# A decoder step on one Trainium2 core: the layer norm's offset added where Z is read, a pair's finish in two steps, four output jobs together

## The chip, the core and the metric

The kernel runs on one core of one Trainium2 chip. Its time is device microseconds of one execution; the profile is of one execution more. TensorE multiplies, VectorE and ScalarE read its results out of PSUM (eight banks of 128 x 512 fp32) and prepare the operands, GpSimd and SyncE issue transfers.

## The reference, cut to what matters

A trunk of two layers over 544 tokens: 512 of a prompt and 32 of eight samples. Each layer is an FFN, a mixer (retention in layer 0, an RG-LRU in layer 1) and a second FFN, and after each of the three stands a layer norm with scale and offset.

```python
def swiglu(x, w_in, w_out):
    g, u = jnp.split(x @ w_in, 2, axis=-1)
    return (jax.nn.silu(g) * u) @ w_out
...
    for layer in range(DEPTH):
        x = layer_norm(ALPHA * x + 0.5 * swiglu(x, ffn1_w_in[layer], ffn1_w_out[layer]),
                       ln_g[layer, 0], ln_b[layer, 0])
        ...  # m = retention (layer 0) or RG-LRU (layer 1)
        x = layer_norm(ALPHA * x + m, ln_g[layer, 1], ln_b[layer, 1])
        x = layer_norm(ALPHA * x + 0.5 * swiglu(x, ffn2_w_in[layer], ffn2_w_out[layer]),
                       ln_g[layer, 2], ln_b[layer, 2])
```

D_MODEL is 1024, D_FF 2816, ALPHA the fourth root of 4; everything is fp32.

## The kernel before

**Layout.** Everything lies transposed: features on the partitions, tokens along the free axis, in two halves of 272 tokens. x has 8 chunks of 128 features. `Z` holds x in fp32; `X`, in the large tile BIG, holds it as a high and a low f32r part (`X[:, 0]`, `X[:, 1]`). A product is three matmuls (`mm3`, line 359): high by high, weight's low by high, high by x's low. Weights come in blocks of 128 x 1024 fp32 (eight tiles) by DMA into one of six `raw` buffers; ScalarE copies the high part into an `hl` buffer and VectorE writes the low part (a split, `split`). There are six `hl` buffers; two more places (`ext`) serve only the plain jobs named below.

**Order of work.** The Python program keeps a clock of its own for TensorE, ScalarE and VectorE (`Flow`, `fl`). Work for the last two is written as generators that yield an event or a time; the next of them to be due is issued when TensorE's planned time passes it. `pace()` is such a time: TensorE's now, or 0.8 us before the later of the other two is through with what it has. So the order of the instructions on each engine is fixed when the program is built, and every engine then runs its own list in that order. `pump` puts in weight splits as buffers come free and blocks have landed.

**An FFN** (`ffn`, called with g = 0, 2, 3 and 5; the two mixers are g = 1 and 4) cuts the 22 chunks of its hidden size into three parts of 8, 8 and 6. The first four chunks of part 0 are plain jobs: gate and up products of each half of the tokens, `ev_g` and `ev_u` read them out of PSUM. All further chunks go in pairs of two chunks by two halves with seven products where eight would be plain (`pair`): the forms s1, a11, s2, a12, s3, s4, a22, in this order, each for gate (i = 0) and up (i = 1), 12 matmuls for each i. The forms s1, s2, s3 and a22 multiply sums and differences of the blocks of x; `sums()` makes them from `Z`, in 1088-wide steps (4 chunks of 272). The generator `ev` combines the products as they end, in the tiles GT and UT (four stretches of 272: chunk j half 0, chunk j half 1, chunk j+1 half 0, chunk j+1 half 1) and RT. `finish` then takes SiLU of the last three stretches of GT in one instruction (816 wide), multiplies with UT in another, and writes the high and low part of both chunks of the hidden state H, 1088 wide each. `hf` says that this is done; the next pair waits for it before it writes GT and UT again.

**Output jobs.** After the pairs of a part come its 16 output jobs, one for each chunk m of x and each half: 8 (in part 2: 6) products over the part's chunks of H. `gangs(jobs, 2)` runs the first two of them interleaved, a product of one, then of the other; all others run alone. `zev` reads a job's bank and adds it to `Z`: in part 0 as ALPHA * Z + bank. In part 2 the job of m = 0 also gives a shift, the sum over chunk 0 of Z (two fp32 matmuls at line 363 for each half), and `prep` subtracts it from the other seven chunks; sums for mean and variance then follow job by job, and `ln` normalises a half after its last job. In part 2 the last four chunks of half 0 come before those of half 1 (in the last FFN, seven), so that half 1's jobs run beside half 0's norm.

**The norm's end.** `ln` writes Z * scale * rstd to `Z`, then with the offset added the two parts of `X`, chunk by chunk. Behind that, for g = 1, 2, 3 and 5, a loop adds the offset to `Z` itself, with a ScalarE instruction for each chunk and half (lines 685 to 691, the event `xf`) and a `pace()` before each. `sums()` of an FFN waits for all 16 of these, and part 0's `zev` for that of its chunk.

`lru_rates` makes the RG-LRU's rates out of `lam`: a few operations of 10 columns on ScalarE, one of them an Exp, and some 30 on VectorE. It stands ahead of FFN 3 and comes due 60 us after that.

Of the kernel before, what the change touches and what calls it, by code (L numbers as in the profile page):

```python
# [27 lines left out]
KC = DM // P  # L28
T = 512
# [174 lines left out]
def build(tc, D, O):  # L204
# [42 lines left out]
    def ccol(name, i=0, w=1, rows=P):  # L247
        return CT[0:rows, CC[name] + i:CC[name] + i + w]

    ident = ccol("ident", 0, P)  # L250
# [139 lines left out]
    def pace():  # L390
        return max(fl.pe, max(fl.dve, fl.act) - 0.8)
# [216 lines left out]
    def ln(li, half, g, final, dep, flush):  # L608
# [75 lines left out]
        fl.set(("lnd", g, half), fl.pe)  # L684
        if not final and g != 4:

            for c in range(KC):
                yield pace()
                z = Z[:, c, sl]
                t = act(z, z, dep=fl.ev["x", g, c, half], func=AF.Identity, bias=pcol("ln_b", 8 * li + c))  # L690
                fl.set(("xf", g, c, half), t)

    def zev(m, half, first, last, lnargs, count, guard=()):
# [4 lines left out]
        def prep(first):  # L698

            for c in range(1, KC):  # L700
                z = Z[:, c, sl]
                if first:
                    t = act(z, f(X[:, 0, c, sl]), scale=ALPHA)
                    stt(z, f(X[:, 1, c, sl]), ALPHA, z, ALU.mult, ALU.add, dep=t)
                else:
                    yield ("zp", g, c, half)
                tt(z, z, L.SH[:, sl], ALU.subtract)
                fl.set(("zd", g, c, half), fl.dve)
                yield pace()
# [26 lines left out]
        def ev(b, t):  # L736
# [10 lines left out]
            if first and not last:  # L747
                yield ("xf", g - 1, m, half)
                t = stt(z, z, ALPHA, b[:, :HF], ALU.mult, ALU.add, dep=t)
                release(b, t)  # L750
            elif first and not m:
                t = stt(z, f(X[:, 0, m, sl]), ALPHA, b[:, :HF], ALU.mult, ALU.add, dep=t)
                release(b, t)
                t = stt(z, f(X[:, 1, m, sl]), ALPHA, z, ALU.mult, ALU.add)
            else:
                t = tt(z, z, b[:, :HF], ALU.add, dep=t)
                release(b, t)
# [85 lines left out]
    def ffn(l, w, g, final=False, extra=None):  # L843
# [47 lines left out]
        def sums():  # L891

            yield ("lnd", g, 1) if g else 0.0
            for c in range(KC):
                for half in range(2):
                    yield ("xf", g, c, half)
            o = LNB[g].o
            T = ar(o, 3, HK * HF).rearrange("p i (c n) -> p i c n", c=HK)
            b11, b12, b21, b22 = (Z[:, k:k + HK, h * HF:h * HF + HF] for k in (0, HK) for h in (0, 1))

            def parts(name, src, hi, lo, t):
# [4 lines left out]
            t = tt(T[:, 0], b11, b12, ALU.subtract)  # L906
            t1 = tt(T[:, 1], b12, b22, ALU.subtract)
            parts("s1", T[:, 0], TF[:, 0, 0], TF[:, 0, 1], t)
            yield pace()
            t = tt(T[:, 2], b11, T[:, 1], ALU.subtract)  # L910
            parts("s2", T[:, 2], TF[:, 1, 0], TF[:, 1, 1], t)
            yield pace()
            parts("s3", T[:, 1], TF[:, 2, 0], TF[:, 2, 1], t1)
            yield pace()
            t = tt(T[:, 0], b21, T[:, 2], ALU.subtract)
            yield ("plain", nin)
# [10 lines left out]
        def pair(j, units_of, p):  # L927
# [6 lines left out]
            def ev(form, i, b, t):  # L934
# [17 lines left out]
                elif form == "s3":  # L952
                    yield ("rd", nin, j, "s4", i)
                    t = tt(B1[i], b, B1[i], ALU.subtract, dep=t)
                    fl.set(("rd", nin, j, "a22", i), t)
                elif form == "a22":
                    t = tt(A1[i], b, R[i], ALU.subtract, dep=t)
# [22 lines left out]
            def finish():  # L980
                for i in range(2):
                    for k in ("c12", "c21"):
                        yield (k, nin, j, i)
                    yield ("rd", nin, j, "a22", i)
                    if i == 0:
                        ts = act(GT[:, HF:], GT[:, HF:], dep=fl.ev["c21", nin, j, 0], func=AF.Silu)
                yield ("h11", nin, j)
                t = stt(UT[:, HF:], UT[:, HF:], 0.5, GT[:, HF:], ALU.mult, ALU.mult, dep=ts)
                hh, hl = H[:, 0, c:c + 2], H[:, 1, c:c + 2]
                u2 = UT.rearrange("p (c n) -> p c n", c=2)  # L990
                t = act(hh, u2, dep=t)
                t = tt(hl, u2, f(hh), ALU.subtract, dep=t)
                for m in (j, j + 1):
                    for half in range(2):
                        fl.set(("h", nin, m, half), t)
                fl.set(("hf", nin, j), t)
# [48 lines left out]

        if extra:
            do(extra)
        do(lambda: st.update(ext=(2, 3)))
        do(lambda: fl.spawn(sums()))
        for hf, (j0, j1) in enumerate(PARTS):  # L1050
# [14 lines left out]
            for m, half in ab(list(range(KC)), (7 if final else 4) if hf == 2 else 0):  # L1065
                def rhs(k, half, j0=j0):
# [3 lines left out]
                                zev(m, half, hf == 0, hf == 2, (li, g + 1, final), count, guard)))  # L1070
            gangs(jobs, 2)

# [525 lines left out]
    def lru_rates():  # L1598
# [5 lines left out]
        def gen():  # L1604
            yield fl.pe + 60
            act(e, lam, func=AF.Abs)
# [208 lines left out]
    with tc.manual_schedule():  # L1815
        def load():
# [22 lines left out]
            def xsplit(c, half, dep):  # L1839
# [3 lines left out]
                fl.set(("x", 0, c, half), t)  # L1843
                fl.set(("xf", 0, c, half), t)
            for c in range(KC):
# [8 lines left out]
            def rest():  # L1854
# [8 lines left out]
                for c in range(KC):  # L1863
                    xsplit(c, 1, 0.0)
                    yield pace()
            fl.spawn(rest())
        load()
# [110 lines left out]
```

## Time and profile before

| | |
|---|---|
| median of 3 runs | 2351.94 us (2349.43 to 2356.76) |
| profiled execution, its own time | 2353.06 us |
| its span, first to last instruction | 2351.3 us |
| TensorE busy | 2289.0 us, 97% |
| VectorE busy | 1532.3 us, 65% |
| ScalarE busy | 1021.0 us, 43% |
| mean granted TensorE clock | 0.991 |

The span is what the trace shows; the profiled execution's own time has 1.8 us more around it. Times in the rows below are microseconds from the span's start. A bracket behind a row of a timeline holds the idle time ahead of it on that engine, and what ended it. The half and the full clock are 0.5 and 1 in the column of the granted clock.

### The profile page before, as it was taken

What the parts mean: (1) busy time and instruction counts of PE and PEld (TensorE: products, weight loads), DVE (VectorE), ACT (ScalarE), POOL (GpSimd) and SP (SyncE); (2) the same over time, 40 slices, a digit from 0 to 9 for tenths busy, and PEclk for the clock granted to TensorE, in tenths of its full rate; (3) what the DMA queues carried; (4) which work ended last, traced back from release to release, by engine and by line L of the source; (5) the groups of instructions that cost most, each with busy time, mean ns of one, the idle gap of its engine ahead of it and who ended that gap; (6) DMA issues with size and microseconds to landing.
All of it is one profiled execution on the core that took longest, in us unless ns stands there. A gap on an engine that the chain in (4) does not pass through costs nothing.

```text
span 2351.3 us, 41831 instructions
## 1 busy us (share of the span) xinstructions
PE 2289.0 (97%) x17530; PEld 2238.5 (95%) x17530; DVE 1532.3 (65%) x2630; ACT 1021.0 (43%) x1557; POOL 143.5 (6%) x195
## 2 busy tenths in 40 slices
PE   9999999999999999999999989999999999999997
PEld 9999999989899998999999989999999999999996
DVE  6647368776766677764636865564787678646367
ACT  5424244442434335533424453333458846424243
POOL 0011000000000000001110000101011000011000
PEclk9999999999999999999999989999999999999998
DMA  7667562153342544466756336665412233657551
GB/s 218 180 140 178 118 178 73 57 174 120 134 159 99 167 144 135 107 162 140 193 113 165 91 84 159 160 172 126 135 59 90 90 108 97 179 117 186 126 139 39
DMA packets 89485, 312.29 MB, mean 133 GB/s; under 512 B 9760, under 2 KB 13856, under 8 KB 89296
## 3 DMA queue, kind: packets, MB, share of 16 engines
q1 hardware_dynamic: 68016, 232.06, 30.0%
q0 software_dynamic: 21280, 77.56, 19.4%
q8 instruction: 137, 2.24, 0.4%
q14 instruction: 52, 0.43, 0.1%
HBM read 288.29 MB, written 21.29 MB: 132 GB/s over the span
## 4 chain that ended last, share of the span: by engine, by line
PE 89%; DVE 7%; ACT 3%; issue 1%; DMA 0%; SPq 0%; ACTq 0%; DVEq 0%
PE bank L359 87%; DVE hl L320 1%; PE bank L363 1%; ACT hl L301 1%; ACT BIG L301 1%; DVE ARF L320 1%; DVE BIG L320 1%; DVE ARF L324 1%; DVE Z L324 1%; DVE Z L320 1%; ACT ARF L301 0%; DVE ARF L329 0%; DVE BIG L324 0%; DVE SM L338 0%; PE bank L367 0%
## 5 line engine op out<-in xcount | busy, mean ns | idle before, releaser
L359 PE MATMUL bank<-BIG,hl 128*128 128x272 f32 x15096 | 1949.7, 290 | 44.0 <-ACT BIG L301 18.9
L359 PEld LDWEIGHTS bank<-BIG,hl 128*128 128x128 f32 x15096 | 1920.5, 189 | 63.9 <-ACT BIG L301 22.7
L320 DVE TENSOR_TENSOR hl<-raw,hl 128x1024 fp32r<-128x1024 f32 (+1 forms) x490 | 596.1, 1221 | 493.6 <-ACT hl L301 491.0
L301 ACT ACTIVATE hl<-raw 128x1024 fp32r<-128x1024 f32 (+1 forms) x490 | 514.1, 1055 | 751.3 <-PE bank L359 572.1
L301 ACT ACTIVATE BIG<-ARF 128x272 fp32r<-128x272 f32 (+11 forms) x198 | 124.0, 638 | 231.9 <-DVE ARF L324 136.5
L464 POOL DMA_DIRECT2D raw<-in_win x144 | 125.5, 899 | 1425.5 <-DVE hl L320 756.5
L320 DVE TENSOR_TENSOR BIG<-ARF,BIG 128x272 fp32r<-128x272 f32 (+11 forms) x198 | 136.6, 702 | 103.2 <-ACT BIG L301 102.6
L320 DVE TENSOR_TENSOR ARF<-bank,ARF 128x272 f32<-128x272 f32 (+3 forms) x460 | 186.0, 436 | 14.6 <-PE bank L363 7.9
L359 PE MATMUL bank<-BIG 128*128 128x272 f32 (+5 forms) x1172 | 194.1, 316 | 0.2 <-DVE ARF L329 0.2
L359 PEld LDWEIGHTS bank<-BIG 128*128 128x128 f32 (+3 forms) x1172 | 167.9, 188 | 13.8 <-DVE ARF L329 0.7
L320 DVE TENSOR_TENSOR Z<-Z,bank 128x272 f32<-128x272 f32 (+1 forms) x238 | 115.0, 491 | 63.4 <-PE bank L359 55.1
L359 PE MATMUL bank<-hl,BIG 128*128 128x256 f32 (+2 forms) x1024 | 146.6, 300 | 2.7 <-ACT BIG L301 1.9
L301 ACT ACTIVATE ARF<-bank 128x272 f32<-128x272 f32 (+5 forms) x278 | 108.9, 400 | 82.6 <-PE bank L359 42.1
L359 PEld LDWEIGHTS bank<-hl,BIG 128*128 128x128 f32 (+1 forms) x1024 | 127.3, 179 | 13.9 <-ACT BIG L301 2.1
L301 ACT ACTIVATE ARF<-Z 128x272 f32<-128x272 f32 (+1 forms) x86 | 39.4, 458 | 103.8 <-DVE Z L320 101.1
L320 DVE TENSOR_TENSOR ARF<-ARF 128x272 f32<-128x272 f32 (+1 forms) x146 | 61.4, 445 | 3.4 <-ACT ARF L301 1.4
L301 ACT ACTIVATE BIG<-Z,PR 128x272 fp32r<-128x272 f32 x80 | 40.8, 521 | 40.6 <-DVE Z L324 40.6
L320 DVE TENSOR_TENSOR Z<-Z,ARF 128x272 f32<-128x272 f32 (+1 forms) x116 | 50.4, 473 | 9.5 <-ACT ARF L301 9.0
L301 ACT ACTIVATE ARF<-ARF 128x272 f32<-128x272 f32 (+1 forms) x79 | 48.3, 631 | 0.4
L324 DVE SCALAR_TENSOR_TENSOR Z<-Z,bank 128x272 f32<-128x272 f32 x80 | 34.3, 434 | 20.4 <-PE bank L359 20.2
L324 DVE SCALAR_TENSOR_TENSOR raw<-raw,bank 128x512 f32<-128x512 f32 x64 | 41.0, 682 | 9.0 <-PE bank L359 9.0
L324 DVE SCALAR_TENSOR_TENSOR ARF<-ARF,PR 128x512 f32<-128x512 f32 (+1 forms) x92 | 40.6, 497 | 9.2 <-ACT ARF L301 9.0
(79 smaller groups left out, 665.0 us busy)
## 6 DMA issues: line engine op xcount, KB each, us to landing
raw<-in_win SPq DMA_DIRECT2D x173, 512.0 KB, 4.3
raw<-in_win POOLq DMA_DIRECT2D x144, 512.0 KB, 5.7
raw<-in_wout SPq DMA_DIRECT2D x88, 512.0 KB, 4.4
raw<-in_sret SPq DMA_DIRECT2D x32, 512.0 KB, 3.6
out_rets<-raw SPq DMA_DIRECT2D x32, 512.0 KB, 5.1
raw<-in_rwin_v SPq DMA_DIRECT2D x16, 512.0 KB, 3.6
raw<-in_rwin_kq SPq DMA_DIRECT2D x16, 512.0 KB, 4.0
raw<-in_rwin_g SPq DMA_DIRECT2D x16, 512.0 KB, 4.7
```

The source lines that it names most:

```text
L301: nc.scalar.activation(out=out, in_=in_, func=func, scale=scale, **kw)
L320: nc.vector.tensor_tensor(out=out, in0=a, in1=b, op=op)
L324: nc.vector.scalar_tensor_tensor(out=out, in0=a, scalar=s, in1=b, op0=op0, op1=op1)
L359: nc.tensor.matmul(out, lhsT=a, rhs=b, start=start, stop=stop, skip_group_check=cont)
L363: nc.tensor.matmul(out, lhsT=a, rhs=b, start=start, stop=stop)
L464: nc.gpsimd.dma_start(out=u["raw"], in_=ap, accum_op=ALU.add)
```

## The change

`Z` now stays without the offset. `offsets()` fills a new tile LB at the start with ALPHA times each norm's offset, and with the offset's chunks 0 to 3 minus its chunks 4 to 7. Whoever reads `Z` adds what is missing: `prep` and the m = 0 job of part 2 ALPHA times the offset (`alb`), `sums()` the offset or the difference, chunk by chunk in instructions of 272 columns (`minus`). The 16 instructions at the end of `ln` and the event `xf` are gone; `sums()` waits for the end of the norm.

`finish` has two steps. The first, when c12 is there (after s4), makes half 1 of chunk j, and with half 0 its two parts of H, 544 columns wide. The second, when c21 and c22 are there (after a22), does the same for chunk j+1. `gangs` interleaves four output jobs in place of two. `lru_rates` is put between the pairs and the output jobs of part 0, and comes due 12 us after that.

```diff
         return CT[0:rows, CC[name] + i:CC[name] + i + w]
+    LB = sbt("LB", 72)
+    def offsets():
+        lb = PR[:, PC["ln_b"]:PC["ln_b"] + 48]
+        tsc(LB[:, 0:48], lb, ALPHA, ALU.mult)
+        l3 = lb.rearrange("p (l a c) -> p l a c", l=6, a=2)
+        tt(LB[:, 48:72].rearrange("p (l c) -> p l c", l=6), l3[:, :, 0], l3[:, :, 1], ALU.subtract)
+    def alb(g, c):
+        return LB[:, 8 * (g - 1) + c:8 * (g - 1) + c + 1]
...
         fl.set(("lnd", g, half), fl.pe)
-        if not final and g != 4:
-            for c in range(KC):
-                yield pace()
-                z = Z[:, c, sl]
-                t = act(z, z, dep=fl.ev["x", g, c, half], func=AF.Identity, bias=pcol("ln_b", 8 * li + c))
-                fl.set(("xf", g, c, half), t)
...
                     yield ("zp", g, c, half)
-                tt(z, z, L.SH[:, sl], ALU.subtract)
+                if first or g == 1:
+                    tt(z, z, L.SH[:, sl], ALU.subtract)
+                else:
+                    stt(z, z, alb(g - 1, c), L.SH[:, sl], ALU.add, ALU.subtract)
                 fl.set(("zd", g, c, half), fl.dve)
...
             if first and not last:
-                yield ("xf", g - 1, m, half)
                 t = stt(z, z, ALPHA, b[:, :HF], ALU.mult, ALU.add, dep=t)
...
                 t = stt(z, f(X[:, 1, m, sl]), ALPHA, z, ALU.mult, ALU.add)
+            elif last and not m and g > 1:
+                t = stt(z, z, alb(g - 1, 0), b[:, :HF], ALU.add, ALU.add, dep=t)
+                release(b, t)
             else:
...
-            yield ("lnd", g, 1) if g else 0.0
-            for c in range(KC):
-                for half in range(2):
-                    yield ("xf", g, c, half)
+            yield ("lnd", g, 1) if g else ("x", 0, KC - 1, 1)
             o = LNB[g].o
...
             b11, b12, b21, b22 = (Z[:, k:k + HK, h * HF:h * HF + HF] for k in (0, HK) for h in (0, 1))
+            c0 = 8 * (g - 1)
+            def minus(out, x, bias, y):
+                if not g:
+                    return tt(out, x, y, ALU.subtract)
+                for c in range(HK):
+                    i = 48 + HK * (g - 1) + c
+                    s = LB[:, i:i + 1] if bias < 0 else pcol("ln_b", c0 + bias + c)
+                    t = stt(out[:, c], x[:, c], s, y[:, c], ALU.add, ALU.subtract)
+                return t
...
             t = tt(T[:, 0], b11, b12, ALU.subtract)
-            t1 = tt(T[:, 1], b12, b22, ALU.subtract)
+            t1 = minus(T[:, 1], b12, -1, b22)
             parts("s1", T[:, 0], TF[:, 0, 0], TF[:, 0, 1], t)
             yield pace()
-            t = tt(T[:, 2], b11, T[:, 1], ALU.subtract)
+            t = minus(T[:, 2], b11, 0, T[:, 1])
             parts("s2", T[:, 2], TF[:, 1, 0], TF[:, 1, 1], t)
...
             yield pace()
-            t = tt(T[:, 0], b21, T[:, 2], ALU.subtract)
+            t = minus(T[:, 0], b21, HK, T[:, 2])
             yield ("plain", nin)
...
                     fl.set(("rd", nin, j, "a22", i), t)
+                    fl.set(("c22", nin, j, i), t)
                 elif form == "a22":
...
             def finish():
-                for i in range(2):
-                    for k in ("c12", "c21"):
-                        yield (k, nin, j, i)
-                    yield ("rd", nin, j, "a22", i)
-                    if i == 0:
-                        ts = act(GT[:, HF:], GT[:, HF:], dep=fl.ev["c21", nin, j, 0], func=AF.Silu)
-                yield ("h11", nin, j)
-                t = stt(UT[:, HF:], UT[:, HF:], 0.5, GT[:, HF:], ALU.mult, ALU.mult, dep=ts)
-                hh, hl = H[:, 0, c:c + 2], H[:, 1, c:c + 2]
-                u2 = UT.rearrange("p (c n) -> p c n", c=2)
-                t = act(hh, u2, dep=t)
-                t = tt(hl, u2, f(hh), ALU.subtract, dep=t)
-                for m in (j, j + 1):
+                for k, sl in ((("c12",), slice(HF, TOK)), (("c21", "c22"), slice(TOK, 2 * TOK))):
+                    for i in range(2):
+                        for w_ in k:
+                            yield (w_, nin, j, i)
+                        if i == 0:
+                            ts = act(GT[:, sl], GT[:, sl], dep=fl.ev[k[0], nin, j, 0], func=AF.Silu)
+                    if len(k) == 1:
+                        yield ("h11", nin, j)
+                    t = stt(UT[:, sl], UT[:, sl], 0.5, GT[:, sl], ALU.mult, ALU.mult, dep=ts)
+                    n = len(k) - 1
+                    hh, hl, src = H[:, 0, c + n], H[:, 1, c + n], UT[:, n * TOK:n * TOK + TOK]
+                    t = act(hh, src, dep=t)
+                    t = tt(hl, src, f(hh), ALU.subtract, dep=t)
                     for half in range(2):
-                        fl.set(("h", nin, m, half), t)
+                        fl.set(("h", nin, j + n, half), t)
                 fl.set(("hf", nin, j), t)
...
-        if extra:
-            do(extra)
         do(lambda: st.update(ext=(2, 3)))
...
                                 zev(m, half, hf == 0, hf == 2, (li, g + 1, final), count, guard)))
-            gangs(jobs, 2)
+            if extra and hf == 0:
+                do(extra)
+            gangs(jobs, 4)
...
         def gen():
-            yield fl.pe + 60
+            yield fl.pe + 12
             act(e, lam, func=AF.Abs)
...
                 fl.set(("x", 0, c, half), t)
-                fl.set(("xf", 0, c, half), t)
             for c in range(KC):
...
                     yield pace()
+                offsets()
             fl.spawn(rest())
```

## Rows read from the trace of the kernel before

**Rows 1.** The page, part 1: busy time, share, instructions of each engine.

```profile
PE 2289.0 (97%) x17530; PEld 2238.5 (95%) x17530; DVE 1532.3 (65%) x2630; ACT 1021.0 (43%) x1557; POOL 143.5 (6%) x195
```

**Rows 2.** Waits of TensorE, whole span: total us, times, longest.

```profile
PE bank L359 <- ACT BIG L301: 20.8, 17, 6.7
...
PE bank L359 <- ACT ARF L301: 5.7, 4, 3.2
```

**Rows 3.** The chain that ended last, near 100 us: start, us, piece.

```profile
100.05 1.07 ACT hl L301
...
101.15 1.23 DVE hl L320
...
102.83 1.02 DVE ARF L324
...
105.01 1.30 DVE BIG L320
```

**Rows 4.** Stretches of 50 us: busy time (instructions) of each engine.

```profile
50.00:100.00 50.00, 50.00 (x401) 50.00 (x400) 32.85 (x45) 23.57 (x29) 4.33 (x5) 1.00 0.75 186
```

**Rows 5.** TensorE's timeline at two starts of output jobs: start, us, [idle before].

```profile
105.03 0.39 PE L359 MATMUL bank<-BIG,hl 128*128 128x272 f32 x1 [0.36 <-ACT BIG L301]
106.36 3.92 PE L359 MATMUL bank<-BIG,hl 128*128 128x272 f32 x29 [0.94 <-DVE BIG L320]
...
1287.36 0.39 PE L359 MATMUL bank<-BIG,hl 128*128 128x272 f32 x1 [1.87 <-ACT BIG L301]
```

**Rows 6.** TensorE's timeline where the pairs of FFN 2 and FFN 3 start.

```profile
986.86 33.88 PE L359 MATMUL bank<-BIG,hl 128*128 128x272 f32 x264
...
1382.19 0.60 PE L359 MATMUL bank<-BIG,hl 128*128 128x272 f32 x1 [6.66 <-ACT BIG L301]
1383.52 11.61 PE L359 MATMUL bank<-BIG,hl 128*128 128x272 f32 x71 [0.73 <-DVE BIG L320]
1398.36 13.84 PE L359 MATMUL bank<-BIG,hl 128*128 128x272 f32 x96 [3.24 <-ACT ARF L301]
```

**Rows 7.** ScalarE's timeline in FFN 3.

```profile
1377.08 0.51 ACT L301 ACTIVATE Z<-Z,PR 128x272 f32<-128x272 f32 x1
...
1389.17 0.21 ACT L301 ACTIVATE SM<-SM 128x10 f32<-128x10 f32 x1
```

**Rows 8.** VectorE's timeline, FFN 2 and FFN 3: the subtractions of sums.

```profile
979.34 2.59 DVE L320 TENSOR_TENSOR ARF<-Z 128x1088 f32<-128x1088 f32 x2
...
1379.71 2.48 DVE L320 TENSOR_TENSOR ARF<-Z 128x1088 f32<-128x1088 f32 x2
...
1394.65 1.28 DVE L320 TENSOR_TENSOR ARF<-Z,ARF 128x1088 f32<-128x1088 f32 x1
```

**Rows 9.** TensorE's timeline at the entries of retention and the RG-LRU.

```profile
412.10 0.50 PE L359 MATMUL bank<-hl,BIG 128*128 128x256 f32 x2 [1.90 <-ACT BIG L301]
...
1723.88 0.65 PE L359 MATMUL bank<-BIG,hl 128*128 128x272 f32 x3 [0.85 <-DVE BIG L324]
```

**Rows 10.** Stretches of TensorE alone: busy us (matmuls), granted clock.

```profile
354.70:358.10 3.40, 3.40 (x15) 0.50 0.46 164
...
1383.60:1388.60 5.00, 5.00 (x22) 0.50 0.02 8
```

**Rows 11.** VectorE's timeline, operations of other widths.

```profile
421.13 0.73 DVE L320 TENSOR_TENSOR BIG<-ARF,BIG 128x544 fp32r<-128x544 f32 x1 [0.72 <-ACT BIG L301]
...
1324.47 0.91 DVE L324 SCALAR_TENSOR_TENSOR Z<-Z,PR,ARF 128x272 f32<-128x272 f32 x2
```

**Rows 12.** Stretches of VectorE alone: busy us (instructions), granted clock.

```profile
1353.90:1373.60 19.70, 8.28 (x16) 1.00 0.30 46
...
1290.00:1315.50 25.50, 19.11 (x45) 0.93 0.26 63
...
1689.10:1714.60 25.50, 21.37 (x50) 1.00 0.19 63
```

**Rows 13.** ScalarE's timeline, a weight split before the output jobs of FFN 0.

```profile
97.09 1.06 ACT L301 ACTIVATE hl<-raw 128x1024 fp32r<-128x1024 f32 x1 [1.95 <-PE bank L359]
```

## The prediction

> **What bounds the kernel now.** I read the page first: TensorE is busy for 97% of the span, VectorE 65%, ScalarE 43% [rows 1]. So two things can shorten the kernel: TensorE's idle stretches, and its time at the half clock. The waits of TensorE name the f32r copies that ScalarE writes into BIG as the largest releaser, 20.8 us in 17 waits [rows 2]. TensorE's own timeline then says where the waits are, and three kinds of places hold most of them.
>
> First, the starts of the output jobs. After each part of an FFN the first two jobs stop at the chunks of H that the last pair makes. In parts 0 and 1 they lose 0.36 + 0.94 us. The chain shows why: from the pair's last matmul at 100.03 it goes through a weight split, a PSUM read, the 816-wide product, the 1088-wide copy and the 1088-wide rest, to 106.32 [rows 3]. That is 6.3 us, and the first job wants the chunk after 36 matmuls, 4.5 us at 0.125 us each (401 in 50 us [rows 4]). In part 2 a job has 6 chunks, wants the first late one after 24 matmuls (3.0 us), and loses 1.87 us and the same 0.94 [rows 5]. There are 8 starts of the first kind and 4 of the second.
>
> Second, FFN 3 (the first one of layer 1). TensorE waits 6.66 + 0.73 us at the first pair and 3.24 us at a12 [rows 6]. ScalarE's rows show why: the last `Z<-Z,PR`, which adds the norm's offset to Z, runs at 1377.08, 23 us after the norm's last chunk, because `pace` lets these go one or two at a time behind everything else [rows 7]. sums() waits for all 16 and starts on VectorE at 1379.71, when the pairs already wait [rows 8]. The 3.24 us is the read of a11 on ScalarE, behind a copy that waits for VectorE's last subtraction of sums, and this began at 1394.65, after the small operations of lru_rates, whose Exp had ended at 1389.4 [rows 7, 8].
>
> Third, the layer norms at the entries of retention and the RG-LRU [rows 9].
>
> [...]
>
> **The change, part by part.** *Output starts.* With four jobs together, chunk k is first wanted after 12k matmuls: at 9.0 and 10.5 us for the two late chunks of parts 0 and 1, at 6.0 and 7.5 us in part 2. The split finish shortens the way to them. Its first step waits for nothing of a22, so the first late chunk is made during a22's matmuls. The second does 544 columns in each of three instructions. A VectorE row of that width says 0.73 us [rows 11]; three of these in place of the 3.5 us from 102.83 to 106.32, and the second chunk is ready 5.0 us after the pair. Against 7.5 and 10.5 us that leaves 2.5 us and more, so all twelve stalls go: 8 x 1.30 + 4 x 2.81 = 21.6 us. Either edit alone would do much of this; they don't add up. After three of the four part 2 starts the clock stood at half for some 3.4 us; the row of the first has 15 matmuls, worth 1.9 us [rows 10]. 3 x 1.5 = 4.5 us. Together 26.1 us.
>
> Four jobs need four of eight banks at once. The last pair holds six, but a12's two and s4's two are read before its a22 ends, and two are free. They also need two weight blocks within 0.75 us. Before the start each split begins as TensorE frees a buffer, every 2.96 us [rows 3, 13], so the ring of six is full and both blocks are there. If they were not, a split would cost its 2.3 us, 100.05 to 102.37 [rows 3]. The two blocks are held for 12 us instead of 6, with four more split ahead of need.
>
> *The offset.* 64 ScalarE instructions of 0.51 us go (16 for each of four norms). Only in FFN 3 does a wait hang on them. sums() now starts with the norm's end, near 1354, not at 1379.7. From there to the pairs are 19.7 us, of which VectorE is busy for 8.28 [rows 12]; sums adds one subtraction of 1.28 us, three of 1.73 us (below) and three rests of 1.29 us, 10.3 us in all, its first operand first. It fits; the second and third operand have 5.8 and 11.7 us more while the pairs run. FFN 2 shows the case: sums at 979.34, 14 us ahead of its pairs, and TensorE runs 264 matmuls through their start without a stop [rows 6, 8]. Queued behind sums are the held-back SiLUs of the gate jobs, about 3 us later than now, and TensorE's banks behind them: two jobs take two banks every 6 us, so that is covered; without the cover it would cost those 3 us. So 6.66 + 0.73 us go.
>
> *lru_rates* moves into the output jobs of FFN 3's part 0, 12 us after they begin. Its 5.2 us on VectorE lie there beside jobs that want one PSUM read in 3 us, with eight banks behind them: nothing, or 5.2 us once if that cover were gone. With both gone from there, the a12 wait of 3.24 us goes too. Of the half clock, the 5.00 us with 22 matmuls and 1 us beside them give back 2.7 us, and the stretch after the a12 wait I count as one of part 2, 1.5 us. Together 14.8 us.
>
> *Small ones.* ScalarE's reads into ARF end four waits, 5.7 us, of which 3.24 are counted [rows 2]. The rest stand behind a 1088-wide finish or a late copy of sums. Of these 2.5 us I take 1.0 (bounds 0 and 2.5). The two instructions that fill LB lie under the first FFN's matmuls, and would cost their two short passes on VectorE, under 1 us.
>
> *What comes back.* In part 2 the first read of PSUM for Z now comes 8 us after the start, and the last job of half 0 still ends after 29 us (72 matmuls, 8 jobs of 2.25 us, 2 us for the shift's sums). In these 21 us VectorE must do what it did in 25.5: 21.37 us in FFN 3, 19.11 in FFN 2 [rows 12], much the same in FFN 0, and in the first two 14 adds with a column, some 0.07 us longer each. FFN 3 is over by 1.3 us; the others may be late by half of that, for the work doesn't come evenly. Late next is the norm, and with it the entries of [rows 9], which have no slack. I take 2.5 us, between 0 and 9 (three norms 1.5 us late, each with 1.5 us of lowered clock).
>
> [...] Rows first: a 1088-wide subtraction takes 1.28 us; two operations of 272 columns with a column operand take 0.91 us, so four come to 1.73 us, 0.45 us more [rows 8, 11]. [...]
>
> **Sum.** 26.1 + 14.8 + 1.0 - 2.5 = 39.4 us. From the profiled execution's 2353.06 us this leaves 2313.7; the median of the runs is 1.1 us lower, so I say 2313 us.
>
> **Rivals.** *A, the norms take more back.* VectorE falls behind in part 2 and three entries stop for 3 to 4 us each, and the clock falls: 9 to 14 us back, 2320 to 2325 us. For it: the 21.37 us above, and entries that stall already. Against it: weight splits can be put off, and the last norm has seven jobs as cover.
>
> *B, FFN 3's wait stays.* The pairs then wait for weight blocks where they waited for sums, and 14.8 us don't come: 2328 us. This is the case in which the new offset does not do its work. Against it: FFN 2.
>
> *C, VectorE bounds the sums.* The smaller instructions delay the first operand in three FFNs, 1.4 us each, with lowered clocks up to 9 us: 2317 to 2322 us. Against it: the 19.7 us with 8.28 busy.
>
> *D, slower.* The second weight block is not there when four jobs start. It decides where the block comes 0.75 + 39.4 / 12 = 4.0 us after every start: beyond that the kernel is slower, at 5 us by 12 us (2364 us). One missed split, 2.3 us, would not reach that. Against it: the full ring.
>
> *E, more.* The entry of retention loses 1.90 us and more [rows 9], then clock; a norm that ends a little sooner there gives 5 us: 2303 to 2308 us.
>
> **How the numbers follow.** Forecast, 2308 to 2318: 0.60. A 0.17, C 0.06, B 0.07, E 0.05, D 0.03, and 0.02 that several things cancel. The range 2303 to 2330 holds all but D, the last, and some of the tails of A and E. A measurement of this kernel tells 0.3%, 7 us, from no change. Only D and the last fall outside faster: faster 0.95, same 0.02, slower 0.03.
>
> **What would show it.** Right: no gap of TensorE at the twelve starts; sums on VectorE within 2 us of the norm's end; no gap at FFN 3's pairs; lru_rates among output jobs; a half clock only at the start, at the entry of retention and at the end. Wrong: a gap early in the output jobs that ends with a weight split (D), longer gaps at the entries with VectorE never idle before them (A), or a gap at the pairs that a split ends (B).

## The result and the profile after

The changed kernel takes 2315.85 us (median of 4 runs, 2314.62 to 2316.85), the kernel before 2353.05 us on the same chip (4 runs, 2349.43 to 2356.76): a ratio of 0.9842 with an interval of 0.9824 to 0.9859. The span of the profiled executions fell from 2351.3 to 2315.1 us, by 36.2 us.

The page, part 1, of the changed kernel, and then its waits of TensorE (releaser, us in total, times, longest), which answer to [rows 1, 2]:

```profile
PE 2273.5 (98%) x17530; PEld 2230.4 (96%) x17530; DVE 1540.3 (67%) x2731; ACT 999.2 (43%) x1564; POOL 143.7 (6%) x195
```

```profile
PE bank L372 <- ACT BIG L314: 14.3, 6, 4.2
...
PE bank L376 <- ACT ARF L314: 1.8, 1, 1.8
```

The matmuls are the same 17530. The f32r copies of ScalarE still hold TensorE for 14.3 us, but in 6 waits where there were 17, so the ones that are left are long. TensorE's timeline of the changed kernel shows where: a start of output jobs in FFN 0's part 0 (with [rows 5]), FFN 3's pairs (with [rows 6]), and the three entries, the first matmuls of the phase that follows a part 2: retention, FFN 3 and the RG-LRU (the first and the last with [rows 9]).

```profile
95.75 12.47 PE L372 MATMUL bank<-BIG,hl 128*128 128x272 f32 x98
...
1365.74 34.51 PE L372 MATMUL bank<-BIG,hl 128*128 128x272 f32 x273
...
386.89 0.80 PE L372 MATMUL bank<-hl,BIG 128*128 128x256 f32 x2 [4.16 <-ACT BIG L314]
...
1310.09 0.62 PE L376 MATMUL bank<-ARF,CT 128*128 128x272 f32 x2
1314.87 0.60 PE L372 MATMUL bank<-BIG,hl 128*128 128x272 f32 x1 [4.16 <-ACT BIG L314]
1316.18 6.02 PE L372 MATMUL bank<-BIG,hl 128*128 128x272 f32 x31 [0.72 <-DVE BIG L337]
...
1696.25 0.60 PE L372 MATMUL bank<-BIG,hl 128*128 128x272 f32 x1 [4.15 <-ACT BIG L314]
```

The start and the pairs are one piece without a stop, and so are the other starts. In their place the three entries wait 4.16, 4.16 and 4.15 us. Before, FFN 3's entry had lost 0.27 us; retention's had lost its 1.90 us at its second half, and that wait is gone now. Behind such a wait the granted clock is lower for a while: it was 0.63 over the 6.8 us from retention's entry, and 0.58 in a stretch of TensorE alone behind FFN 3's (busy us, matmuls, granted clock), which has 25 matmuls in 5.00 us, where 40 fit at 0.125 us each:

```profile
1316.20:1321.20 5.00, 5.00 (x25) 0.58 0.33 66
```

VectorE's timeline at FFN 3's sums (with [rows 8]) follows: the first subtraction follows the norm's last rest without a gap, and the subtraction with a column operand has become four.

```profile
1339.08 1.32 DVE L337 SCALAR_TENSOR_TENSOR BIG<-Z,PR,BIG 128x272 fp32r<-128x272 f32 x3
1340.32 1.28 DVE L333 TENSOR_TENSOR ARF<-Z 128x1088 f32<-128x1088 f32 x1
1341.52 1.73 DVE L337 SCALAR_TENSOR_TENSOR ARF<-Z,LB 128x272 f32<-128x272 f32 x4
```

**Where the 36.2 us came from.** Both traces have the same 17530 matmuls, and as many of them between one of these places and the next, so the time at which the n-th one starts can be compared place by place. An a12 wait is one ahead of that form of a pair.

| place | us saved |
|---|---|
| 8 starts in parts 0 and 1, 1.83 each | 14.7 |
| 4 starts in part 2 (4.9, 5.4, 3.8, 5.0) | 19.0 |
| FFN 3's first pair and a12 | 15.5 |
| smaller a12 waits in FFN 2 and FFN 5 | 3.1 |
| entries of retention, FFN 3, RG-LRU (-0.6, -6.9, -3.7) | -11.2 |
| end of retention (-1.8), the last norm (-2.3), the rest | -5.0 |
| sum | 36.1 |

### The profile page after: what moved, and what is told of

Its sections match the earlier page's. It is cut to its first block, busy times and chain, and to the rows that moved or that the text cites. A ratio compares the mean times of both kernels' runs of the same rounds, so it can differ in the third digit from the quotient of the medians.

```text
span 2315.1 us, 41946 instructions
## 1 busy us (share of the span) xinstructions
PE 2273.5 (98%) x17530; PEld 2230.4 (96%) x17530; DVE 1540.3 (67%) x2731; ACT 999.2 (43%) x1564; POOL 143.7 (6%) x195
## 4 chain that ended last, share of the span: by engine, by line
PE 91%; DVE 4%; issue 3%; ACT 1%; DMA 1%; SPq 0%; POOL 0%; ACTq 0%; POOLq 0%; DVEq 0%
PE bank L372 90%; PE bank L376 1%; DMA raw<-in_win 1%; DVE Z L333 1%; ACT ARF L314 0%; DVE ARF L342 0%; DVE Z L337 0%; DVE hl L333 0%; DVE ARF L333 0%; ACT hl L314 0%; DVE SM L351 0%; PE bank L380 0%; DVE ARF L337 0%; ACT Z L314 0%; DMA Z<-in_x 0%
## 5 line engine op out<-in xcount | busy, mean ns | idle before, releaser
L314 ACT ACTIVATE BIG<-ARF 128x544 fp32r<-128x544 f32 (+11 forms) x234 | 131.1, 571 | 305.0 <-DVE ARF L337 219.5
L333 DVE TENSOR_TENSOR BIG<-ARF,BIG 128x544 fp32r<-128x544 f32 (+10 forms) x234 | 142.3, 618 | 110.2 <-ACT BIG L314 109.7
L372 PEld LDWEIGHTS bank<-BIG 128*128 128x128 f32 (+3 forms) x1172 | 167.7, 188 | 13.7 <-DVE ARF L342 0.7
L314 ACT ACTIVATE ARF<-ARF 128x272 f32<-128x272 f32 x114 | 54.6, 492 | 3.6 <-DVE ARF L333 3.1
L337 DVE SCALAR_TENSOR_TENSOR ARF<-ARF,PR 128x512 f32<-128x512 f32 (+1 forms) x92 | 40.5, 496 | 14.7 <-ACT ARF L314 14.7
L337 DVE SCALAR_TENSOR_TENSOR ARF<-ARF 128x272 f32<-128x272 f32 x84 | 46.7, 556 | 0.4
```

Of the source, the lines that this page charges most:

```text
L314: nc.scalar.activation(out=out, in_=in_, func=func, scale=scale, **kw)
L333: nc.vector.tensor_tensor(out=out, in0=a, in1=b, op=op)
L337: nc.vector.scalar_tensor_tensor(out=out, in0=a, scalar=s, in1=b, op0=op0, op1=op1)
L372: nc.tensor.matmul(out, lhsT=a, rhs=b, start=start, stop=stop, skip_group_check=cont)
```

## The experiments

The starts and FFN 3 are plain. What the runs had to settle is what each part is worth alone, and why the entries now wait. For the second there were two theories. Theory 1: with four jobs together VectorE is handed part 2's first sums late, and is simply behind when the norm comes. Theory 2: weight splits, put off while VectorE is behind, stand in the engines' queues ahead of the norm's steps. VectorE's timeline of the changed kernel at FFN 3's entry spoke for the second, for it idles in front of the norm:

```profile
1300.25 0.49 DVE L337 SCALAR_TENSOR_TENSOR Z<-Z,LB,ARF 128x272 f32<-128x272 f32 x1
1302.52 1.23 DVE L333 TENSOR_TENSOR hl<-raw,hl 128x1024 fp32r<-128x1024 f32 x1 [1.77 <-ACT hl L314]
1303.66 0.43 DVE L333 TENSOR_TENSOR Z<-Z,bank 128x272 f32<-128x272 f32 x1
...
1305.59 2.36 DVE L333 TENSOR_TENSOR hl<-raw,hl 128x1024 fp32r<-128x1024 f32 x2 [0.68 <-ACT hl L314]
1307.87 0.43 DVE L333 TENSOR_TENSOR ARF<-ARF 128x272 f32<-128x272 f32 x1
```

The last read of half 0 (1303.66) stands behind one split, the last sum of squares (1307.87) behind three. The first of them waits for ScalarE, which has just loaded a function table:

```profile
1300.03 1.28 ACT L314 ACT_TABLE_LOAD   x1
1301.33 0.20 ACT L314 ACTIVATE SM<-CT 128x1 f32<-128x1 f32 x1
1301.44 1.04 ACT L314 ACTIVATE hl<-raw 128x1024 fp32r<-128x1024 f32 x1
```

And over the 21 us of part 2 that the prediction worried about, VectorE is busy for 16.42 us, not for all of them (a stretch of VectorE alone):

```profile
1276.50:1297.50 21.00, 16.42 (x39) 1.00 0.32 76
```

### Each part alone

**Four jobs together**, the kernel before with

```
-            gangs(jobs, 2)
+            gangs(jobs, 4)
```

> The kernel before with only this of the change: four output jobs together. Theory (four jobs alone cover the starts, and make the norms late): the eight starts of parts 0 and 1 lose nothing, the four of part 2 at most 0.3 us, 33 us in all with the clock; the norms take some 12 us back; FFN 3's wait stays: about 2332 us. Rival (the finish in two steps is what covers the starts): starts still lose over 1 us each, 2343 us or more.

2332.50 us, ratio 0.9910 (0.9896 to 0.9925). All twelve starts run through, without the split finish. FFN 3's entry already waits as in the changed kernel, with no offset arithmetic on VectorE:

```profile
1314.07 0.62 PE L363 MATMUL bank<-ARF,CT 128*128 128x272 f32 x2
1318.85 0.59 PE L359 MATMUL bank<-BIG,hl 128*128 128x272 f32 x1 [4.16 <-ACT BIG L301]
```

Retention and the RG-LRU wait 4.16 us too. So four jobs make these waits by themselves.

**The finish in two steps**, the kernel before with the changed kernel's `finish()` and two jobs.

> The kernel before with only the finish in two steps; two jobs together, offset and lru_rates as before. Theory (the two steps shorten the way to H by 1.3 us and free its first chunk early): parts 0 and 1 lose 0.4 us instead of 1.3 at a start, part 2 1.4 + 0.4 us instead of 1.9 + 0.9, as the run with all but the four jobs showed; 14 us in all, FFN 3's wait stays: about 2339 us. Rival (the finish is held by the weight split ahead of it, not by its own width): 2348 us or more.

2343.26 us, 0.9952 (0.9934 to 0.9970). TensorE's timeline at the start near 100 us has one stop left of two:

```profile
104.51 2.65 PE L359 MATMUL bank<-BIG,hl 128*128 128x272 f32 x19 [0.37 <-DVE BIG L320]
```

In part 2 a start keeps 1.37 and 0.37 us. FFN 3's 6.66 + 0.73 us stay, and 3.9 us are lost in retention.

**The offset added where Z is read**, with lru_rates at its old place:

```
-            for c in range(KC):
-                yield pace()
-                z = Z[:, c, sl]
-                t = act(z, z, ..., func=AF.Identity, bias=pcol("ln_b", 8 * li + c))
...
+                    t = stt(out[:, c], x[:, c], s, y[:, c], ALU.add, ALU.subtract)
```

> The kernel before with only the offset added where Z is read; lru_rates stays at the start of FFN 3, two jobs, finish in one step. Theory (sums waited for the 16 offset instructions): the 6.7 + 0.7 us at FFN 3's pairs go with most of the half clock, the wait at a12 stays because of lru_rates: about 2342 us. Rival (weight blocks are as late as sums): 2350 us or more.

2343.71 us, 0.9962 (0.9949 to 0.9974). FFN 3's first pair no longer waits; later reads there stop TensorE for 2.47 and 0.81 us, and by the end of the pairs 9.5 us are gained against before.

**The same, and lru_rates moved:**

```
-        if extra:
-            do(extra)
...
+            if extra and hf == 0:
+                do(extra)
```

> The kernel before with the offset added where Z is read and lru_rates moved to the output jobs; two jobs, finish in one step. Theory: all of FFN 3's waits go, 15.5 us as between the two kernels: about 2337 us. Rival (lru_rates is covered in either place): the same as the run with the offset alone, within 2 us.

2345.92 us, 0.9968 (0.9954 to 0.9981): no better than without the move. The profiled execution of this run was its fastest and that of the run before its slowest (2341.89 and 2349.11 us), so place by place tells more. At FFN 3's pairs the trace gains 14.8 us against before, then 5.9 us go to waits of the same pairs on later reads, which leaves 8.9 for the 9.5 without the move; 3.5 us go at the RG-LRU's entry.

The gains of the parts are 20.4 us (jobs), 8.8 (finish) and 6.2 (offset with lru_rates), 35.4 us in all; together they gave 37.2. They add up in sum, but not place by place. With four jobs alone no start stops any more, so the finish has little left to do there; FFN 3's pairs still stop for 5.31, 1.28 and 0.54 us in that run, and 9.5 us of what the other parts then add come there.

### What the entries wait for

**Two jobs again**, in the changed kernel:

```
-            gangs(jobs, 4)
+            gangs(jobs, 2)
```

> The changed kernel with two output jobs together instead of four; all else of the change stays. Theory (four jobs late in part 2 crowd the norm): the norms' waits at the three entries fall back from 4.2 + 0.7 us to under 2 us and their half clock goes; the twelve starts are mostly covered by the finish in two steps, parts 0 and 1 lose under 0.5 us, part 2 about 1.2 us each. Time about 2310 us. Rival (the norms are late for another reason, the column adds or the offset): the three waits stay at 4 us and more and part 2 loses 1.2 us each on top, about 2322 us.

2330.83 us, 0.9904 (0.9889 to 0.9918), slower than either expected. FFN 3's entry is down to 0.28 us as meant. But each start stops for 0.37 us or more, and FFN 3's pairs stop again, for a new reason. ScalarE's timeline there:

```profile
1375.35 2.00 ACT L314 ACTIVATE hl<-raw 128x1024 fp32r<-128x1024 f32 x2 [1.33 <-DMA raw<-in_win]
1377.26 0.38 ACT L314 ACTIVATE ARF<-bank 128x272 f32<-128x272 f32 x1
...
1388.02 2.00 ACT L314 ACTIVATE hl<-raw 128x1024 fp32r<-128x1024 f32 x2 [7.46 <-DMA raw<-in_win]
```

The splits at 1375.35 wait 1.33 us for their weights to land, and the read of PSUM behind them, at 1377.26, ends a stop of TensorE of 3.09 us. Those at 1388.02 wait 7.46 us; VectorE's reads queue behind its part of them, and TensorE stops for 2.57 us.

**Two jobs in part 2 alone:**

```
-            gangs(jobs, 4)
+            gangs(jobs, 2 if hf == 2 else 4)
```

> The changed kernel with four jobs together in parts 0 and 1 and two in part 2. Theory: no loss at the eight starts of parts 0 and 1, about 1.2 us at the four of part 2, norms' waits back under 2 us with full clock: about 2308 us, the fastest of the two-job versions. Rival: norms' waits stay at 4 us and more, about 2321 us.

2323.34 us, 0.9873 (0.9856 to 0.9889). So four jobs are worth 7.5 us in parts 0 and 1, and another 7.5 us in part 2 net of the entries.

**Three jobs in part 2** (`gangs(jobs, 3 if hf == 2 else 4)`), to start VectorE's sums sooner without a stop:

> The changed kernel with three output jobs together in part 2 (both halves of m = 0 and one of m = 1), four in parts 0 and 1. With three, the late chunks of H are wanted after 36 and 45 matmuls, 4.5 and 5.6 us, and are there at 5.0 us at the latest, so the starts stay without a loss, and VectorE gets the shift 2.2 us sooner. Theory 1 (VectorE's lateness holds the norms): the three waits of 4.2 + 0.7 us shrink by 2 us each, 2308 to 2311 us. Theory 2 (the weight splits that the planner puts before the norm's end hold it): the waits stay, 2313 to 2318 us.

2315.97 us, 0.9838 (0.9824 to 0.9853), the changed kernel's time. The three waits are 4.16 us each. This does not speak against theory 1 as it seems to. At FFN 3's entry the last sum of squares is ready 2.1 us before TensorE comes to the float32 matmul that wants it, against 1.8 in the changed kernel, but that matmul still stands behind all output jobs, and as long as it does the wait cannot fall (see the table below).

**No split during a norm unless it is due** (5.0 us of lead while a norm runs, in place of 11.5):

```
-            if u["off"] - st["main"] > LEAD and (st["crit"] or ...
+            if u["off"] - st["main"] > (5.0 if st["crit"] else LEAD) and (st["crit"] or ...
```

> The changed kernel, with one number of the planner changed: while a norm runs, a weight block is split only if it is wanted within 5 us of work, not 11.5. This moves three splits that stand between the last output job of half 0 and the end of its norm behind the norm. Theory (three splits of 1.2 us on VectorE hold the norm up): the three waits of 4.2 + 0.7 us shrink by 3.5 us each, the half clock after them mostly goes: 2300 to 2305 us. Rival (the norm's own operations are late, the splits only fill gaps): the waits shrink by under 1.5 us each, 2312 us or more; or the blocks come late at the entries, same time as the changed kernel.

2356.20 us, 1.0015 (1.0005 to 1.0024): the whole gain is gone. The entry waits fall only to 1.90 to 2.29 us, and the weight blocks come too late, with stops of 6.57 us in FFN 2, 11.46 in FFN 3 and 10.96 in FFN 5. TensorE's timeline in FFN 3:

```profile
1361.08 0.82 PE L372 MATMUL bank<-BIG,hl 128*128 128x272 f32 x2 [11.46 <-ACT hl L314]
```

**Two splits ahead of the jobs.** Around part 2 two splits are made at the start, where VectorE has room (lead 30 us), and none is issued until the norm's steps stand in the queues:

```
+            if st["hold"]:
+                break
-            if u["off"] - st["main"] > LEAD and (...
+            if u["off"] - st["main"] > max(LEAD, st["early"]) and (...
...
```

> The changed kernel, but two weight splits are made at part 2's start, and no split is then put on an engine until the norm's steps stand in the queues. Theory (splits queued ahead of the norm's reads and square sum hold it): the three waits of 4.16 us at the entries of retention, FFN 3 and the RG-LRU fall to 1.5 us or less each, and most of the 6.8 us at half clock behind each goes: 8 to 16 us off, 2300 to 2308 us, ratio to the kernel before 0.977 to 0.981. Rival (the time was only lent: the splits that are now later hold the first weight blocks, or the pairs of the phase that begins): the entry waits shrink, but waits at second weight blocks or at FFN 3's pairs take it back, 2313 us or more.

2317.08 us, 0.9857 (0.9842 to 0.9873). The mechanism moved and the time did not: the three waits are 1.90, 2.67 and 2.66 us, and FFN 3's pairs stop for 0.71 and 1.95 us, the second block of retention's half 1 for 0.81. **The same without the ban:**

> As the run before, without the ban: two splits are made at part 2's start, and the others go where the planner puts them. Theory: one or two splits fewer stand ahead of the norm, so the three waits fall from 4.16 us to 2 to 3 us each, 2308 to 2313 us. Rival (splits due later simply move up into the places that came free): the waits stay 4.16 us, 2314 to 2317 us.

2316.99 us, 0.9856 (0.9841 to 0.9871). The waits are 4.16 us: two splits still stand around the last sum, later ones that moved up. At FFN 3's entry the sum of squares is ready 3.1 us before TensorE comes to it. **The first of these with three jobs in part 2:**

> As the first of these, with three output jobs together in part 2 in place of four. Theory of the splits: as the first run within 2 us, since the number of jobs did not move the entry waits before. Rival (with the splits out of the way VectorE's lateness is what holds the norm): 2 to 6 us better than the first run.

2318.10 us, 0.9862 (0.9845 to 0.9878); waits 2.66, 3.40, 3.41 us. At FFN 3's entry VectorE no longer idles before the last read in the first of these three runs, yet that read comes at 1302.42, only 1.2 us sooner than in the changed kernel, of which TensorE is 0.8 us ahead at part 2's start already: the two splits moved ahead seem to cost VectorE the time that they had cost behind. But VectorE is not what the norm waits for then. VectorE's timeline of the first of the three:

```profile
1304.01 0.43 DVE L333 TENSOR_TENSOR ARF<-ARF 128x272 f32<-128x272 f32 x1
1307.29 0.72 DVE L333 TENSOR_TENSOR Z<-Z,bank 128x544 f32<-128x544 f32 x1 [2.85 <-ACT ARF L314]
```

Its last sum of squares is done at 1304.44, and it idles for 2.85 us. TensorE comes to the two float32 sums of this norm at 1306.20 and 1307.78, without a stop ahead of either: they stand that late in its order.

**The splits made cheap.** The last run leaves work out: between part 2's start and the norm, the split's rest is computed for 64 of 1024 columns:

```
+            for w in [slice(0, 64)] if short else parts:
                 t = tt(hl[:, 1, w], raw[:, w], f(hl[:, 0, w]), ALU.subtract, ...
...
```

> The changed kernel, with one piece of work left out: for the weight blocks split between part 2's start and the norm's end at the three entries (some four each), VectorE subtracts only 64 of 1024 columns, so some 1.1 us less each. ScalarE's part of each split stays. Theory (VectorE's share of these splits, wherever it is put, is what the entries pay): the three waits fall from 4.16 to 1.9 us or less, nothing comes back downstream, 2298 to 2308 us. Rival 1 (ScalarE's part in front of the norm's reads, or four jobs that end together, holds the norm): waits stay above 3 us, 2311 to 2316 us. Rival 2 (as with the moved splits, the gain is lost again at FFN 3's pairs): waits fall, but 2312 us or more.

2313.57 us, 0.9836 (0.9822 to 0.9850). The waits fall: none at retention's first half, 1.53 and 1.54 us at the others. Retention's second half, which did not wait in the changed kernel, waits 1.90 us again. FFN 3's entry is reached 6.8 us sooner than in the changed kernel, 1308.04 for 1314.87; 4.0 us of this TensorE had before that norm. Some 770 matmuls later, behind the pairs, 1.8 us are left. ScalarE's timeline before FFN 3's pairs, first of the changed kernel, then of this one, shows why:

```profile
1372.95 2.01 ACT L314 ACTIVATE hl<-raw 128x1024 fp32r<-128x1024 f32 x2 [0.69 <-DMA raw<-in_win]
```

```profile
1372.94 3.91 ACT L314 ACTIVATE hl<-raw 128x1024 fp32r<-128x1024 f32 x4 [1.71 <-DMA raw<-in_win]
```

The weights are there at 1372.9 in both, though TensorE is 7.1 us ahead in this kernel. That is no fixed moment: the same split starts at 1371.36 with three jobs in part 2 and at 1377.23 with two splits ahead and the ban. Its transfer adds one block onto another that has just been split, and GpSimd issues it some 0.3 us after VectorE is through with that earlier split, in each of these four kernels (0.29 in the changed one). GpSimd's timeline of the changed kernel, then of this one:

```profile
1367.27 0.86 POOL L477 DMA_DIRECT2D raw<-in_win  x1 [4.63 <-DVE hl L333]
```

```profile
1365.77 0.87 POOL L478 DMA_DIRECT2D raw<-in_win  x1 [7.64 <-DVE hl L333]
```

So the earlier split came only 1.5 us sooner here, and the transfer then took 1.5 us longer. In this kernel four splits then go first, and VectorE reads the pairs' products after them; VectorE's and TensorE's timelines:

```profile
1374.04 4.63 DVE L333 TENSOR_TENSOR hl<-raw,hl 128x1024 fp32r<-128x1024 f32 x4 [4.33 <-ACT hl L314]
1378.58 0.43 DVE L337 SCALAR_TENSOR_TENSOR ARF<-bank,ARF 128x272 f32<-128x272 f32 x1
```

```profile
1379.51 15.35 PE L372 MATMUL bank<-BIG,hl 128*128 128x272 f32 x120 [1.17 <-DVE ARF L333]
1396.85 3.46 PE L372 MATMUL bank<-BIG,hl 128*128 128x272 f32 x18 [1.99 <-DVE ARF L333]
```

So even with most of VectorE's share of these splits taken away for nothing, the kernel gains some 2 us, which is no more than these runs can tell. Rival 2 of the expectation holds. Between the two theories this run does not decide: it takes the splits from ahead of the norm, and it also takes work off VectorE.

**What sets the size of an entry wait** can be read from one number, the count of matmuls that TensorE still has behind the norm's last float32 sum. TensorE's timeline at FFN 3's entry in the kernel before:

```profile
1319.19 0.62 PE L363 MATMUL bank<-ARF,CT 128*128 128x272 f32 x2
1319.45 6.13 PE L359 MATMUL bank<-BIG,hl 128*128 128x272 f32 x46
1325.84 1.34 PE L359 MATMUL bank<-BIG,hl 128*128 128x272 f32 x8 [0.27 <-DVE BIG L324]
```

and in the run with two splits ahead and the ban:

```profile
1307.78 0.62 PE L376 MATMUL bank<-ARF,CT 128*128 128x272 f32 x2
1308.04 1.86 PE L372 MATMUL bank<-BIG,hl 128*128 128x272 f32 x12
1312.56 0.39 PE L372 MATMUL bank<-BIG,hl 128*128 128x272 f32 x1 [2.67 <-ACT BIG L314]
```

| matmuls behind the last sum | wait, us | 4.16 - 0.125 x matmuls |
|---|---|---|
| 45 (before; the row's 46th is the next phase's first) | 0 | below 0 |
| 21 (two jobs in part 2; splits cheap) | 1.53 | 1.54 |
| 18 (retention's second half, before) | 1.90 | 1.91 |
| 15 (no split during a norm) | 2.29 | 2.29 |
| 12 (two splits ahead, ban) | 2.67 | 2.66 |
| 6 (the same, three jobs) | 3.40 | 3.41 |
| 0 (changed; four jobs alone) | 4.16 | 4.16 |

From the last sum to the first block is a fixed chain, some 4.2 us longer than the sum. All that a late norm costs is the matmuls that no longer lie beside it, 45 of them at FFN 3's entry in the changed kernel.

In none of these runs does TensorE wait for that sum itself: at the three entries its input is ready 1.4 to 3.9 us before TensorE comes to it. So the size of a wait is set by the place that the program gave the sum in TensorE's order. That is why the wait is 4.16 us in the changed kernel and in three of the runs, whatever was moved: the sum stands behind the last output job in all of them. VectorE's work, splits among it, can count here only through the planner's clock, by which that place was chosen; the planner's times are in no trace, so this step is read from the program and not shown.

## Why the prediction came out as it did

The forecast was 2313 us and the kernel takes 2315.85. The mechanisms of the gains were right. Two of the four terms were badly mis-sized in opposite directions, by 7.6 and 13.7 us, so the nearness of the sum is largely luck.

- *Output starts, 26.1 us.* All twelve are gone, as worked out; they gave 33.7. The term counted idle time. But a stop also costs what the matmul before it takes to end: a lone one lasts 0.39 us against 0.125 in a row, so 0.265 us more for each stop. 0.36 + 0.94 + 2 x 0.265 is 1.83, what was measured; in part 2, 2.81 + 0.53 is 3.34, and with 1.5 us of clock at three of four starts the term would have been 8 x 1.83 + 4 x 3.34 + 4.5 = 32.5 us. That either edit would do much of it holds for four jobs; the finish alone leaves 0.37 and more at each start.
- *FFN 3, 14.8 us.* The 2.7 us of half clock in this term are an estimate: 45% of 6 us, since 22 matmuls took 5.00 us at a granted clock of 0.50, where at 0.125 us each they take 2.75. Measured 15.5 in all, and by the mechanism named: sums at the norm's end, four subtractions in 1.73 us, no stop at the pairs, where 273 matmuls now take 34.51 us at a granted clock of 1.00. Less right is what was said of lru_rates: moved on top of the offset alone it gained nothing, since the pairs then stopped a little later on other reads, and the two edits together kept 8.9 us at this place. It takes the other parts of the change to keep the 15.5.
- *Small ones, 1.0 us (0 to 2.5).* 3.1 us at a12 in FFN 2 and FFN 5, above the bound.
- *What comes back, 2.5 us (0 to 9).* The entries took 11.2 us, and another 5.0 us, which no term held, went at retention's end, at the last norm and in small places. That is 16.2 us, beyond the bound of 9. This is the step that failed, and rival A is what happened: "three entries stop for 3 to 4 us each, and the clock falls". The places, the waits (4.2 us) and the lowered clock (0.58 behind FFN 3's) came as A described, by themselves 11.2 us in place of 2.5. Its cause is only half as told: VectorE is busy for 16.42 of the 21 us and idles just ahead of the norm. And what the prediction held against A, "weight splits can be put off", is part of it: put off, they come together ahead of the norm's last read and sum, and where most of VectorE's share of them was left out, 21 to 42 matmuls came back beside the chain. What the term lacked is the cover: it priced a norm by its lateness, 1.5 us, and not by the matmuls that lie beside its end. The last norm's seven jobs of cover lie beside its half 0; the 2.3 us went at its half 1, 0.4 of them ahead of its sums and 1.9 behind them, for a cause that stays open.
- *Rivals B, C, D, E* did not come, in the changed kernel. B's place, a split that holds FFN 3's pairs, is where the gain goes in nearly every run that shortens the entries. For C, the four instructions take 1.73 us where one took 1.28, as the rows had it, 0.45 us more and three times that, some 1.4 us, in a sums(), which has room for them. For D, no start waits for a weight block.

What stays open: how much of the entries' loss could be had back. The runs show that it is not had by moving splits, since FFN 3's pairs then stop for weights whose load follows other splits; whether those splits could come earlier was not tried. Nor was a norm's float32 sum placed sooner in TensorE's order. In the changed kernel the last sum of squares at FFN 3's entry is ready at 1308.30 and TensorE comes to it at 1310.09: those 1.8 us are 14 matmuls, with which the table above gives an estimated wait of 2.4 us for the 4.16. No version ran measurably faster than the changed kernel.

## What to carry to other kernels

Price a stop of TensorE as its idle time plus the longer end of the matmul ahead of it plus the slow stretch behind it, each from a row; here the idle time was 2.81 us and the longer ends 0.53 of some 4.9 us. Where a stage starts sooner because its predecessor no longer stops, ask what was done for free in the stop: here splits, reads and loads used it, and at FFN 3's entry a split that waited for ScalarE left VectorE idle for 1.77 us ahead of the norm's last read. Before blaming the engine that a wait names, count the work that the program's order puts beside the chain: where nothing lies beside it, the wait is at its ceiling (4.16 us here), and a test that leaves it unmoved says little. One event at the same time in two traces may be chance; look at it in a third, and at what issued it.

## What the runs showed that was not expected

- A wait that grows by exactly the cover it loses, 0.125 us for each matmul, and ends at 4.16 us, the same at three entries of three different phases, while the sum that it starts from is never waited for.
- The load of a function table on ScalarE takes 1.28 us and stands ahead of a weight split that needs both engines, for which VectorE idles 1.77 us ahead of the norm's last read. The last 0.56 us of the load lie in these 1.77; the rest is mostly the copy of the split.
- Of the 6.9 us lost at FFN 3's entry, 4.6 are idle time (4.16 + 0.72 against 0.27 before) and 0.27 the longer matmul of one stop more; the other 2.1 are left for the lowered clock behind it, where 25 matmuls took 5.00 us at 0.58.
